# Multiplying each weight slab with both token tiles by turns, with PSUM divided four and four

## The chip, the cores and the metric

The kernel runs on one core of one Trainium2 chip. The metric is the device time of one execution in microseconds (us); less is better.

## The reference

Two transformer blocks over 256 tokens of width 2048, in float32, batch 1. Cut to what matters here:

```
# block 1
h = rms_norm(x);  proj = h @ w_in                       # 7 parts of 1024 columns
o_da = differential_attention(q, k, v)                  # 8 heads, 2 score maps each
o_hg = hgrn2(f, q, i, g)                                # gated linear attention, 8 heads
x = x + rms_norm(concat(o_da, o_hg) @ w_out)
x = x + rms_norm(cross_attention(x, mem) @ w_co)        # 4 heads, 256 memory tokens
x = x + rms_norm((silu(h @ w_gate) * (h @ w_up)) @ w_ffn_out)          # hidden 5632
# block 2
z = rms_norm(x) @ w_in_2                                # pool, q, k, v, gate, r, branch gates
y_a = pool_mixer(p) @ w_branch_a;  y_b = (rms_norm(gla(q, k, v, a)) * silu(r)) @ w_branch_b
x = x + rms_norm((sigmoid(g0) * y_a + sigmoid(g1) * y_b) @ w_out_2)
x = x + rms_norm((silu(h @ w_ffn_gate) * (h @ w_ffn_up)) @ w_ffn_down) # hidden 5632
```

Nearly all work is a product of 256 tokens with a weight matrix that is read once from HBM.

## The kernel before

The 256 tokens are two token tiles of 128, called t = 0 and t = 1 (`NT` is 2). A product is cut into **groups** of 512 weight columns (`group`). A group's weights come in **slabs** of 256 rows by 512 columns (`wsub`): SyncE loads a slab of 512 KB into one of 4 buffers `raw`, ScalarE rounds it to `wh` (line 375), VectorE forms the remainder `wl = raw - wh` (line 376). `wh` and `wl` have 8 buffers each (`SPLIT_BUFS`), so a group over 2048 rows, which is 8 slabs, fills them all. The activations are held transposed and divided in the same way, `hi` and `lo`. TensorE then adds three products for each 128 rows: hi by wh (line 401), hi by wl (402), lo by wh (403); the activation tile is the stationary operand and 512 weight columns stream.

In `mm` one token tile runs over all slabs of the group, then the other: a **pass** for t = 0 and a pass for t = 1, each with a PSUM buffer of its own from the pool `psm` (2 buffers). All other products and transposes take PSUM from the pool `pss` (6 buffers). A slab is free only when the second pass has gone over it.

When a pass is over, a consumer takes the product out of PSUM: `u_in` (line 887, VectorE) multiplies up by silu(gate) into `hh`, `channel` copies to `tok`, `b_in` (lines 1050, 1051) forms the gated branch sum. Most consumers then transpose their tile with 4 products by the identity (line 304, tile `tp`). These steps are generators; `tick`, called after every 6 products of a pass, moves each a step, so that a transpose is written some 6 products behind the pass whose result it takes. The attention parts run in the same way as background jobs between the products.

Engines follow the order in which the tile scheduler places instructions on each; the weights of a group get a priority 50 instructions ahead (`AHEAD`), and none ahead behind a normalisation (`self.bound`, `BOUNDARY_AHEAD`). TensorE, ScalarE and VectorE each take their instructions strictly in that order.

Of the kernel before, what the change touches and what calls it, by code (L numbers as in the profile page):

```python
# [81 lines left out]
class Builder:  # L82
    def __init__(self, ctx, tc, A, out):
        self.tc, self.nc, self.A, self.out = tc, tc.nc, A, out
        e = ctx.enter_context
        self.cp = e(tc.tile_pool(name="const", bufs=1))
        self.ap = e(tc.tile_pool(name="acts", bufs=ACT_UNITS))
        self.rawp = e(tc.tile_pool(name="raw", bufs=RAW_BUFS))
        self.spp = e(tc.tile_pool(name="split", bufs=SPLIT_BUFS))
        self.smp = e(tc.tile_pool(name="small", bufs=16))  # L90
        self.psm = e(tc.tile_pool(name="psm", bufs=2, space=bass.MemoryType.PSUM))
        self.pss = e(tc.tile_pool(name="pss", bufs=6, space=bass.MemoryType.PSUM))
        self.n = 0
        self.junk = self.cp.tile([P, CW], F32, name="junk")
        self.jobs, self.lane, self.bound = [], [], False

# [210 lines left out]
    def split_T(self, ps, gcol=None, same=False):  # L307
        """two float32r parts of ps, each channel times its gain in column gcol (+ i for tile i)."""
        nc = self.nc
        hi, lo = self.uT("hi"), self.uT("lo")  # L310
        if gcol is None:
            nc.scalar.copy(hi, ps)
            nc.vector.tensor_tensor(lo, ps, hi.bitcast(F32), ALU.subtract)
            return hi, lo
        if same:
            g = self.vec[:, gcol:gcol + 1]
            nc.scalar.activation(hi, ps, AF.Copy, scale=g)
            nc.vector.scalar_tensor_tensor(lo, ps, g, hi.bitcast(F32), ALU.mult, ALU.subtract)
            return hi, lo
        for i in range(4):  # L320
            g = self.vec[:, gcol + i:gcol + i + 1]
            nc.scalar.activation(hi[:, i, :], ps[:, i, :], AF.Copy, scale=g)  # L322
            nc.vector.scalar_tensor_tensor(lo[:, i, :], ps[:, i, :], g, hi[:, i, :].bitcast(F32), ALU.mult, ALU.subtract)  # L323
        return hi, lo
# [10 lines left out]
    def token(self, dst, scale):  # L335
        """consumer: token-major, times the token's scale."""
# [6 lines left out]
    def channel(self, dst, scale):  # L343
        """consumer: the same, transposed in float32."""
# [11 lines left out]
    def sigmoid_(self, x):  # L356
        """1/(1+exp(-x)) for an SBUF or PSUM operand, and 1+exp(-x)."""
# [9 lines left out]
    def wsub(self, W, k0, c0, ncol=CW):  # L367
        """256 rows of a weight chunk, split exactly into two float32r parts."""
# [10 lines left out]
    def ahead(self):  # L379
        """weights of a group are prepared before the work emitted just before it; less so behind a boundary."""  # L380
# [4 lines left out]
    def group(self, W, c0, hT, ks, consume, k_off=0, ncol=CW):  # L385
        """out[t] = h[t] @ W[:, c0:c0+ncol] over the k tiles `ks` (even, in pairs)."""
        with self.ahead():
            subs = [(k, self.wsub(W, k + k_off, c0, ncol)) for k in ks[::2]]
        for t in range(NT):
            self.mm(t, subs, hT, consume, ncol)  # L390
# [28 lines left out]
    def normed(self, start, pre):  # L419
        """spawns per token tile: start(t) yields chunks of x; they are transposed, times the gain, and split.  # L420
        Returns rstd and hT, filled as the jobs run."""
# [22 lines left out]
    def residual(self, gain, x, n_chunks=4):  # L444
        """consumers that collect ps*gain and the sum of squares; done(t) yields the chunks of
        x + ps * gain / rms, in the place of ps*gain."""
# [25 lines left out]
    def boundary(self, start, pre):  # L472
        """start(t) -> chunks of the new x, consumed when the last product of tile t is in."""
# [11 lines left out]
    def decay_attn(self, qT, kT, bT, v, esc, cph, dv, store):  # L485
        """qT/kT/bT: per token tile [128 ch, 4, 128]; cph channel tiles per head;
        v(t, head) -> [128 tok, dv]; store(t, h0, ps) takes the outputs."""
# [94 lines left out]
    def head_norm(self, po, nh):  # L582
        """each head of po [128 tok, nh x dv] over its rms; gains are left to the transpose."""
# [15 lines left out]
    def hgrn(self, g, W, hT, rstd, mixT):  # L599
# [42 lines left out]
        self.group(W, 3072 + CW * g, hT, ks, f_in)  # L642
# [80 lines left out]
    def block1(self, x_src):  # L723
# [69 lines left out]
        self.group(A["w_cq"][0], 0, hT, ks, q_in)  # L793
# [60 lines left out]
    def chunks(self, W, hT, ks, cons, job):  # L854
        """all four column chunks of a product with a boundary behind it."""
        for n in range(4):
# [6 lines left out]
            self.group(W, n * CW, hT, ks, g)  # L863

    def ffn(self, x, rstd, hT, Wg, Wu, Wd, post):
        """the feed-forward block; returns done(t), the products of its last consumer, to be given a job."""
# [6 lines left out]
        def run(job):  # L873
            for bi, (b0, nb) in enumerate(blocks):
                hid = [[None] * nb for _ in range(NT)]
                last = bi == len(blocks) - 1
                for c in range(nb):
# [14 lines left out]
                    self.group(Wg, (b0 + c) * CW, hT, ks, g_in)  # L892
# [3 lines left out]
                for n in range(4):  # L896
# [17 lines left out]
                    self.group(Wd, n * CW, hid, list(range(4 * nb)), d_in, k_off=4 * b0)  # L914
        return run, lambda t: self.add_normed(y[t], acc[t], x[t])

# [1 line left out]
    def block2(self, ffn1):  # L918
# [33 lines left out]
        def r_in(a, b, skip):  # L952
            """columns a..b of r, behind `skip` columns of something else."""
# [65 lines left out]
        self.group(W, 5120, hT, ks, gl_in, ncol=416)  # L1019
# [121 lines left out]
```

## Time and profile before

| | |
|---|---|
| time, median of 3 runs | 2907.09 us (2901.22 to 2908.91) |
| span of the profiled execution | 2903.0 us |
| PE (TensorE products) busy | 2844.2 us, 98% |
| PEld (weight loads of TensorE) busy | 2350.3 us, 81% |
| DVE (VectorE) busy | 1616.9 us, 56% |
| ACT (ScalarE) busy | 1412.9 us, 49% |
| moved by DMA | 530.93 MB, mean 183 GB/s |

The profile shows one execution, whose span runs from its first to its last instruction; the time of an execution measured by itself is in the first row, and the span of the profiled one lies within the spread of those. Each engine's row is the time in which it had an instruction in work. A product on PE stands with a modelled end: rows overlap where products are pipelined, so that the pace is read from the starts of rows that follow each other, and an idle time on PE is counted from the modelled end.

### The profile page before, as it was taken

How to read it: one execution, taken by the hardware profiler on the slowest of the kernel's cores; microseconds unless marked ns; L12 is line 12 of the kernel's file. 1: busy time of each engine (PE TensorE's matmuls, PEld its weight loads, DVE VectorE, ACT ScalarE, POOL GpSimd, SP SyncE). 2: the span in 40 equal slices, each digit the busy share in tenths (PEclk: the TensorE clock that was granted, in tenths of full speed). 3: DMA queues.
4: the chain of work that ended last, by engine and by line, in shares of the span. 5: the costliest groups of instructions: out<-in, count | busy, mean ns of one | idle time of the engine just before them, and what ended most of it. 6: DMA issues, size and time to landing. Idle time of an engine off the chain costs nothing.

```text
span 2903.0 us, 35034 instructions
## 1 busy us (share of the span) xinstructions
PE 2844.2 (98%) x13196; PEld 2350.3 (81%) x13196; DVE 1616.9 (56%) x2147; ACT 1412.9 (49%) x2100; POOL 44.8 (2%) x89
## 2 busy tenths in 40 slices
PE   8999999999999999999999999999999999999998
PEld 6788888778888888888888898887887888888887
DVE  6666585664544455447565565555565445444555
ACT  6455584664443443445555475344464344443443
POOL 1000000000000000000000000000000000000000
PEclk9999999999999999999999999999999999999999
DMA  7554456445556556655555446655656556555663
GB/s 227 160 181 159 157 176 206 163 150 182 185 199 196 174 177 204 198 190 192 180 169 165 150 144 212 205 178 178 230 160 214 190 175 191 193 192 177 194 207 136
DMA packets 274921, 530.93 MB, mean 183 GB/s; under 512 B 17513, under 2 KB 29413, under 8 KB 274752
## 3 DMA queue, kind: packets, MB, share of 16 engines
q1 hardware_dynamic: 269040, 512.70, 54.2%
q0 software_dynamic: 5136, 14.95, 1.7%
q8 instruction: 103, 1.69, 0.2%
q10 hardware_dynamic: 576, 1.05, 0.1%
q14 instruction: 66, 0.54, 0.1%
HBM read 522.86 MB, written 5.77 MB: 182 GB/s over the span
## 4 chain that ended last, share of the span: by engine, by line
PE 80%; DMA 7%; DVE 6%; ACT 5%; issue 2%; SPq 0%; ACTq 0%; DVEq 0%
PE mm L401 25%; PE mm L403 25%; PE mm L402 25%; DVE wl L376 3%; ACT wh L375 3%; DMA raw<-w_in 2%; PE tp L304 2%; PE lps L495 1%; DMA raw<-w_ffn_in 1%; DMA raw<-w_ffn_gate 1%; ACT hi L322 1%; ACT junk L299 1%; DVE hh L887 1%; DMA raw<-w_ffn_out 0%; DMA raw<-w_ffn_down 0%
## 5 line engine op out<-in xcount | busy, mean ns | idle before, releaser
L376 DVE TENSOR_TENSOR wl<-raw,wh 128x1024 fp32r<-128x1024 f32 (+1 forms) x968 | 1171.8, 1215 | 728.0 <-ACT wh L375 693.1
L401 PE MATMUL mm<-wh,hi 128*128 128x512 f32 (+2 forms) x3808 | 1497.2, 393 | 6.1 <-ACT hi L322 2.8
L403 PE MATMUL mm<-wh,lo 128*128 128x512 f32 (+2 forms) x3808 | 1482.0, 389 | 0.0
L402 PE MATMUL mm<-wl,hi 128*128 128x512 f32 (+2 forms) x3808 | 1481.6, 389 | 0.0
L375 ACT CAST wh<-raw 128x1024 fp32r<-128x1024 f32 (+1 forms) x968 | 1009.8, 1046 | 793.5 <-PE mm L403 457.7
L401 PEld LDWEIGHTS mm<-wh,hi 128*128 128x128 f32 x3808 | 716.5, 188 | 153.5 <-ACT hi L322 6.7
L403 PEld LDWEIGHTS mm<-wh,lo 128*128 128x128 f32 x3808 | 715.8, 188 | 146.7 <-DVE lo L323 2.1
L402 PEld LDWEIGHTS mm<-wl,hi 128*128 128x128 f32 x3808 | 716.8, 188 | 139.3 <-issue 0.7
L882 ACT ACTIVATE sg<-mm,r 128x512 f32<-128x512 f32 x44 | 30.2, 685 | 168.3 <-PE mm L403 168.3
L887 DVE SCALAR_TENSOR_TENSOR hh<-mm,r,sg 128x512 f32<-128x512 f32 x44 | 32.9, 748 | 131.7 <-PE mm L403 131.7
L333 ACT ACTIVATE tok<-mm,r 128x512 f32<-128x512 f32 x44 | 30.1, 685 | 125.8 <-PE mm L403 125.8
L323 DVE SCALAR_TENSOR_TENSOR lo<-tp,vec,hi 128x128 fp32r<-128x128 f32 x224 | 69.1, 345 | 28.7 <-ACT hi L322 28.1
L322 ACT ACTIVATE hi<-tp,vec 128x128 fp32r<-128x128 f32 x224 | 72.5, 381 | 21.5 <-DVE lo L323 11.5
L906 DVE TENSOR_TENSOR y<-mm,y 128x512 f32<-128x512 f32 x32 | 22.0, 688 | 89.5 <-PE mm L403 89.5
L495 PEld LDWEIGHTS lps<-qd,kd 128*128 128x128 f32 x448 | 58.0, 191 | 4.8 <-DVE qd L522 1.0
L495 PE MATMUL lps<-qd,kd 128*128 128x64 f32 x448 | 56.3, 268 | 0.6 <-DVE qd L522 0.6
L529 DVE COPY_PREDICATED attn<-mask,lps 128x256 f32<-128x256 int32 (+1 forms) x56 | 24.1, 431 | 49.3 <-PE lps L495 49.0
L458 DVE TENSOR_TENSOR mg<-mm,gpost 128x512 f32<-128x512 f32 x24 | 16.5, 686 | 50.2 <-ACT junk L299 50.2
L1042 ACT ACTIVATE gate<-gate 128x512 f32<-128x512 f32 x16 | 10.1, 631 | 68.2 <-DVE gate L1041 68.1
L299 ACT ACTIVATE junk<-mm 128x512 f32<-128x512 f32 x24 | 14.5, 604 | 59.0 <-PE mm L403 59.0
L304 PE MATMUL tp<-ident,hh 128*128 128x128 f32 x176 | 27.6, 279 | 15.2 <-DVE hh L887 15.1
L304 PEld LDWEIGHTS tp<-ident,hh 128*128 128x128 f32 x176 | 20.1, 139 | 27.4 <-DVE hh L887 24.5
(235 smaller groups left out, 1112.8 us busy)
## 6 DMA issues: line engine op xcount, KB each, us to landing
raw<-w_in SPq DMA_DIRECT2D x256, 512.0 KB, 4.6
raw<-w_ffn_in SPq DMA_DIRECT2D x176, 512.0 KB, 4.7
raw<-w_ffn_out SPq DMA_DIRECT2D x88, 512.0 KB, 4.8
raw<-w_ffn_gate SPq DMA_DIRECT2D x88, 512.0 KB, 4.7
raw<-w_ffn_up SPq DMA_DIRECT2D x88, 512.0 KB, 4.7
raw<-w_ffn_down SPq DMA_DIRECT2D x88, 512.0 KB, 4.9
raw<-w_out SPq DMA_DIRECT2D x64, 512.0 KB, 4.9
raw<-w_branch_b SPq DMA_DIRECT2D x32, 512.0 KB, 5.1
```

Source lines behind the costliest of these rows:

```text
L299: self.nc.scalar.activation(self.junk[:, :src.shape[-1]], src, AF.Square, accum_out=acc)
L304: self.nc.tensor.transpose(ps[:, i, :], src[:, i * P:(i + 1) * P], self.ident)
L322: nc.scalar.activation(hi[:, i, :], ps[:, i, :], AF.Copy, scale=g)
L323: nc.vector.scalar_tensor_tensor(lo[:, i, :], ps[:, i, :], g, hi[:, i, :].bitcast(F32), ALU.mult, ALU.subtract)
L375: nc.scalar.copy(hi[:, :, :ncol], raw[:, :, :ncol])
L376: nc.vector.tensor_tensor(lo[:, :, :ncol], raw[:, :, :ncol], hi[:, :, :ncol].bitcast(F32), ALU.subtract)
L401: nc.tensor.matmul(ps[:, :ncol], xh, wh[:, i, :ncol], start=kk == first, stop=False)
L402: nc.tensor.matmul(ps[:, :ncol], xh, wl[:, i, :ncol], start=False, stop=False)
L403: nc.tensor.matmul(ps[:, :ncol], xl, wh[:, i, :ncol], start=False, stop=kk == last)
L495: nc.tensor.matmul(ps[:, h, :], lhs[:, i, :], rhs[:, i, :], start=c == 0, stop=c == cph - 1)
L882: nc.scalar.activation(u, ps, AF.Silu, scale=rstd[t])
L887: nc.vector.scalar_tensor_tensor(u, ps, rstd[t], sg[t], ALU.mult, ALU.mult)
```

## The change

Where `group` ran `mm` twice, it now runs `mm_both`: both token tiles get a PSUM buffer at once, and each slab operand is multiplied with t = 0 and directly after with t = 1. The slab is then done with. Consumers of both tiles are spawned at the end of the group. `tick` still comes after every 6 products. A group keeps the two passes (`apart`) where the second tile's input isn't there yet or a normalisation follows: the first group, the last column group of the products ahead of a normalisation, and the first group behind one. The pool `psm` gets 4 PSUM buffers and `pss` 4. Of 11,616 products with weights, 10,704 are written by `mm_both`.

```
-        self.psm = e(tc.tile_pool(name="psm", bufs=2, space=bass.MemoryType.PSUM))
-        self.pss = e(tc.tile_pool(name="pss", bufs=6, space=bass.MemoryType.PSUM))
+        self.psm = e(tc.tile_pool(name="psm", bufs=4, space=bass.MemoryType.PSUM))
+        self.pss = e(tc.tile_pool(name="pss", bufs=4, space=bass.MemoryType.PSUM))
...
-    def group(self, W, c0, hT, ks, consume, k_off=0, ncol=CW):
+    def group(self, W, c0, hT, ks, consume, k_off=0, ncol=CW, apart=False):
+        apart = apart or self.bound
         with self.ahead():
             subs = [(k, self.wsub(W, k + k_off, c0, ncol)) for k in ks[::2]]
+        if apart:
+            for t in range(NT):
+                self.mm(t, subs, hT, consume, ncol)
+        else:
+            self.mm_both(subs, hT, consume, ncol)
+
+    def mm_both(self, subs, hT, consume, ncol):
+        nc = self.nc
+        ps = [self.psmm() for _ in range(NT)]
+        first, last = subs[0][0], subs[-1][0] + 1
+        for k, (wh, wl) in subs:
+            self.flush(lambda: all(hT[t][k // 4] is not None for t in range(NT)))
+            for i in range(2):
+                kk = k + i
+                for p, w in ((0, wh), (0, wl), (1, wh)):
+                    for t in range(NT):
+                        nc.tensor.matmul(ps[t][:, :ncol], hT[t][kk // 4][p][:, kk % 4, :], w[:, i, :ncol],
+                                         start=kk == first and p == 0 and w is wh, stop=kk == last and p == 1)
+                self.tick()
         for t in range(NT):
-            self.mm(t, subs, hT, consume, ncol)
+            self.spawn(consume(t, ps[t]))
...
-        self.group(W, 3072 + CW * g, hT, ks, f_in)
+        self.group(W, 3072 + CW * g, hT, ks, f_in, apart=g == 0)
...
-            self.group(W, n * CW, hT, ks, g)
+            self.group(W, n * CW, hT, ks, g, apart=n == 3)
```

The same argument is added for the first gate group of a feed-forward block, the last column group of its output product, the query product of the cross attention and the first group of block 2.

On TensorE, where one group ends and the next begins, in the feed-forward block of block 1. Before, this is the end of an up group's second pass (product `mm_1348`), then the first pass of the next gate group (`mm_1377`), and in it the transposes of the tile `hh_1352` that the second pass gave:

```order
L402 MATMUL mm_1348_6228<-wl_1345_6174,hi_1249_5718 128x512
L403 MATMUL mm_1348_6228<-wh_1344_6173,lo_1250_5719 128x512
L401 MATMUL mm_1377_6336<-wh_1354_6290,hi_1184_5450 128x512
L402 MATMUL mm_1377_6336<-wl_1355_6291,hi_1184_5450 128x512
L403 MATMUL mm_1377_6336<-wh_1354_6290,lo_1185_5451 128x512
L401 MATMUL mm_1377_6336<-wh_1354_6290,hi_1184_5450 128x512
L402 MATMUL mm_1377_6336<-wl_1355_6291,hi_1184_5450 128x512
L403 MATMUL mm_1377_6336<-wh_1354_6290,lo_1185_5451 128x512
L304 MATMUL tp_1378_6343<-ident_81,hh_1352_6286 128x128 x4
```

The same place in the changed kernel (`mm_1346` and `mm_1347` are the two tiles of the up group, `mm_1374` and `mm_1375` of the next, `hh_1348` and `hh_1349` what the consumer makes of the first two):

```order
L407 MATMUL mm_1346_6177<-wh_1344_6173,lo_1195_5513 128x512
L407 MATMUL mm_1347_6178<-wh_1344_6173,lo_1250_5719 128x512
L407 MATMUL mm_1374_6327<-wh_1351_6281,hi_1184_5450 128x512
L407 MATMUL mm_1375_6328<-wh_1351_6281,hi_1241_5660 128x512
L407 MATMUL mm_1374_6327<-wl_1352_6282,hi_1184_5450 128x512
L407 MATMUL mm_1375_6328<-wl_1352_6282,hi_1241_5660 128x512
L407 MATMUL mm_1374_6327<-wh_1351_6281,lo_1185_5451 128x512
L407 MATMUL mm_1375_6328<-wh_1351_6281,lo_1242_5661 128x512
L304 MATMUL tp_1376_6335<-ident_81,hh_1348_6275 128x128 x4
L304 MATMUL tp_1377_6340<-ident_81,hh_1349_6277 128x128 x4
```

The transposes still stand 6 products into the next group, but now those of both token tiles, and the products between take each slab operand twice in a row.

On VectorE, around the consumers of the same up group. Before, between the first tile's `hh_1347` and the second's `hh_1352`, with `wl_1355` to `wl_1376` the eight slabs of the next group and `lo` the remainder of a transposed tile:

```order
L887 SCALAR_TENSOR_TENSOR hh_1347_6226<-mm_1346_6177,r_1203_5548,sg_1319_6076 128x512
L376 TENSOR_TENSOR wl_1355_6291<-raw_1353_6288,wh_1354_6290 128x1024
L313 TENSOR_TENSOR lo_1351_6247<-tp_1349_6235,hi_1350_6246 128x512
L376 TENSOR_TENSOR wl_1358_6297<-raw_1356_6294,wh_1357_6296 128x1024
L376 TENSOR_TENSOR wl_1361_6303<-raw_1359_6300,wh_1360_6302 128x1024
L376 TENSOR_TENSOR wl_1364_6309<-raw_1362_6306,wh_1363_6308 128x1024
L376 TENSOR_TENSOR wl_1367_6315<-raw_1365_6312,wh_1366_6314 128x1024
L376 TENSOR_TENSOR wl_1370_6321<-raw_1368_6318,wh_1369_6320 128x1024
L887 SCALAR_TENSOR_TENSOR hh_1352_6286<-mm_1348_6228,r_1256_5750,sg_1321_6127 128x512
L376 TENSOR_TENSOR wl_1373_6327<-raw_1371_6324,wh_1372_6326 128x1024
```

In the changed kernel (`wl_1352` to `wl_1373` are the eight slabs of the next group):

```order
L376 TENSOR_TENSOR wl_1364_6306<-raw_1362_6303,wh_1363_6305 128x1024
L376 TENSOR_TENSOR wl_1367_6312<-raw_1365_6309,wh_1366_6311 128x1024
L376 TENSOR_TENSOR wl_1370_6318<-raw_1368_6315,wh_1369_6317 128x1024
L908 SCALAR_TENSOR_TENSOR hh_1348_6275<-mm_1346_6177,r_1203_5548,sg_1320_6125 128x512
L908 SCALAR_TENSOR_TENSOR hh_1349_6277<-mm_1347_6178,r_1256_5750,sg_1321_6127 128x512
L376 TENSOR_TENSOR wl_1373_6324<-raw_1371_6321,wh_1372_6323 128x1024
L313 TENSOR_TENSOR lo_1379_6352<-tp_1376_6335,hi_1378_6351 128x512
L313 TENSOR_TENSOR lo_1381_6356<-tp_1377_6340,hi_1380_6355 128x512
```

The two consumers now stand side by side, behind seven of the next group's eight slabs; before, six slabs stood between them.

On TensorE in the differential attention of the changed kernel: `atp_715` is a transposed score tile, `aT_716` what ScalarE copies from it, `tp_723` a transposed memory tile; with four buffers in `pss`, `tp_723` takes the PSUM buffer that `atp_715` had.

```order
L714 MATMUL atp_715_3347<-ident_81,sce_661_3171 128x128 x2
L407 MATMUL mm_703_3297<-wh_701_3293,hi_17_148 128x512
L407 MATMUL mm_704_3298<-wh_701_3293,hi_70_357 128x512
L407 MATMUL mm_703_3297<-wl_702_3294,hi_17_148 128x512
L407 MATMUL mm_704_3298<-wl_702_3294,hi_70_357 128x512
L407 MATMUL mm_703_3297<-wh_701_3293,lo_18_149 128x512
L407 MATMUL mm_704_3298<-wh_701_3293,lo_71_358 128x512
L304 MATMUL tp_723_3379<-ident_81,mem_710_3337 128x128 x4
L723 MATMUL dapo_670_3209<-tok_454_2226,aT_716_3350 128x128 x2
```

Six products lie between the last write of the old tile and the first write of the new one. In the program before there are 3 places in `pss` with room for at most 12 products between (other work of TensorE counted by its columns); in the changed one 12.

## Rows read from the trace of the kernel before

**Rows 1.** The page: span, and its first part (busy, share, instructions).
```profile
span 2903.0 us, 35034 instructions
PE 2844.2 (98%) x13196; PEld 2350.3 (81%) x13196; DVE 1616.9 (56%) x2147; ACT 1412.9 (49%) x2100; POOL 44.8 (2%) x89
```
**Rows 2.** Groups of PE by form: count, busy us, mean ns, idle before, releasers.
```profile
L401 PE MATMUL mm<-wh,hi 128*128 128x512 f32 x3648 | 1440.0, 395 | 5.7 <-ACT hi L322 2.4 <-DVE mg L458 1.8 <-ACT wh L375 1.0
```
**Rows 3.** Timeline of PE around a change of pass: start, duration, instruction.
```profile
1012.88 0.39 PE L402 MATMUL mm<-wl,hi 128*128 128x512 f32 x1
1013.10 0.39 PE L403 MATMUL mm<-wh,lo 128*128 128x512 f32 x1
1013.33 0.39 PE L401 MATMUL mm<-wh,hi 128*128 128x512 f32 x1
...
1014.46 0.39 PE L403 MATMUL mm<-wh,lo 128*128 128x512 f32 x1
1014.70 0.60 PE L304 MATMUL tp<-ident,hh 128*128 128x128 f32 x4
```
**Rows 4.** Windows: a first pass and a second pass; busy us of each engine.
```profile
1002.50:1013.50 11.00, 11.00 (x50) 9.13 (x49) 3.67 (x3) 2.83 (x4) 0.00 (x0) 1.00 0.66 222
1013.50:1024.50 11.00, 11.00 (x52) 9.06 (x52) 7.48 (x7) 6.52 (x7) 0.00 (x0) 1.00 0.50 163
```
**Rows 5.** Timeline of ACT in the next second pass; in brackets idle before and releaser.
```profile
1041.10 1.06 ACT L375 CAST wh<-raw 128x1024 fp32r<-128x1024 f32 x1 [0.30 <-PE mm L403]
1042.46 1.06 ACT L375 CAST wh<-raw 128x1024 fp32r<-128x1024 f32 x1 [0.30 <-PE mm L403]
1044.46 1.05 ACT L375 CAST wh<-raw 128x1024 fp32r<-128x1024 f32 x1 [0.95 <-DMA raw<-w_ffn_in]
```
**Rows 6.** Waits of PE, whole span: total us, times, longest.
```profile
PE tp L304 <- DVE hh L887: 15.1, 20, 1.5
...
PE tp L304 <- DVE gate L1051: 4.6, 4, 1.7
PE tp L304 <- DVE sg L946: 3.0, 2, 2.1
...
PE tp L304 <- ACT tok L333: 2.6, 4, 1.1
PE cpo L821 <- ACT tok L333: 2.2, 1, 2.2
...
PE tp L304 <- DVE hn L594: 1.3, 2, 1.1
PE mm L401 <- ACT wh L375: 1.0, 1, 1.0
```
**Rows 7.** Timeline of all engines at the end of an up group's second pass.
```profile
1069.69 1.05 ACT L375 CAST wh<-raw 128x1024 fp32r<-128x1024 f32 x1 [2.39 <-DMA raw<-w_ffn_out]
...
1070.77 1.23 DVE L376 TENSOR_TENSOR wl<-raw,wh 128x1024 fp32r<-128x1024 f32 x1 [2.22 <-ACT wh L375]
...
1071.08 0.39 PE L403 MATMUL mm<-wh,lo 128*128 128x512 f32 x1
...
1071.91 0.74 DVE L887 SCALAR_TENSOR_TENSOR hh<-mm,r,sg 128x512 f32<-128x512 f32 x1
...
1072.71 0.66 PE L304 MATMUL tp<-ident,hh 128*128 128x128 f32 x4 [1.24 <-DVE hh L887]
```
**Rows 8.** DVE timeline, the consumer of a first pass.
```profile
1013.53 0.75 DVE L887 SCALAR_TENSOR_TENSOR hh<-mm,r,sg 128x512 f32<-128x512 f32 x1 [6.70 <-PE mm L403]
```
**Rows 9.** Tile gate: the two steps of the branch sum, ns min/median/max.
```profile
L1050 DVE TENSOR_TENSOR gate<-mm,gate x8: 682/688/691, 1911.4 to 2062.4; 128x512 f32<-128x512 f32 x8
L1051 DVE TENSOR_TENSOR gate<-gate,gate x8: 681/689/693, 1912.1 to 2064.7; 128x512 f32<-128x512 f32 x8
```
**Rows 10.** Waits of TensorE's weight loads: for a copied score tile.
```profile
PEld dapo L702 <- ACT aT L695: 0.9, 3, 0.5
```
**Rows 11.** A window near the start (before the last two columns: granted clock), and PE in it.
```profile
25.00:30.00 5.00, 4.94 (x23) 4.20 (x24) 3.95 (x11) 4.62 (x14) 3.94 (x8) 0.66 0.97 346
...
26.18 0.57 PE L402 MATMUL mm<-wl,hi 128*128 128x512 f32 x1
26.55 0.63 PE L403 MATMUL mm<-wh,lo 128*128 128x512 f32 x1
```

More of the change, by code (lines that the diff above doesn't have):

```diff
@@ L792, in q_in @@
             yield from self.channel(cqT, rq)(t, ps)
-        self.group(A["w_cq"][0], 0, hT, ks, q_in)
+        self.group(A["w_cq"][0], 0, hT, ks, q_in, apart=True)
         oT = [[None] for _ in range(NT)]
@@ L891, in u_in @@
                         yield from self.to_T(u, put)
-                    self.group(Wg, (b0 + c) * CW, hT, ks, g_in)
+                    self.group(Wg, (b0 + c) * CW, hT, ks, g_in, apart=bi == 0 and c == 0)
                     self.group(Wu, (b0 + c) * CW, hT, ks, u_in)
@@ L913, in d_in @@
                                 self.spawn(job(t))
-                    self.group(Wd, n * CW, hid, list(range(4 * nb)), d_in, k_off=4 * b0)
+                    self.group(Wd, n * CW, hid, list(range(4 * nb)), d_in, k_off=4 * b0, apart=last and n == 3)
         return run, lambda t: self.add_normed(y[t], acc[t], x[t])
@@ L1017, in unit @@
                 self.group(W, 3072 + n * CW, hT, ks, self.token(vs[n], rstd))
-        self.group(W, 5120, hT, ks, gl_in, ncol=416)
+        self.group(W, 5120, hT, ks, gl_in, ncol=416, apart=True)
         unit(0)
```

## Prediction

> **What bounds the kernel now.** I read the first part of the page first: PE is busy for 98% of the span, VectorE and ScalarE for about half of it [rows 1]. A product's row lasts 0.39 us while the next one starts 0.23 us later [rows 3], so that busy share counts overlap. The starts tell the pace: from 1012.88 to 1014.46 lie 7 steps, 1.58 us, or 0.226 to 0.227 us for each product of 512 columns. 10,944 of them (3 lines of 3648 [rows 2]) make 0.227 x 10,944 = 2,484 us of a span of 2,903; the rest of the 11,616 are like them, and transposes and attention products come on top. TensorE's own work is therefore the bound, and this change removes none of it. What can be gained is the time in which PE waits, what can be lost are new waits or a slower pace.
>
> So I read the waits of PE next. The largest is that of transposes for `hh`, what VectorE makes of an up product: 15.1 us in 20 places; then `gate` 4.6, `sg` 3.0, `tok` 2.6, one wait of the cross attention 2.2, and for slabs themselves 1.0 [rows 6]. A feed-forward block has 11 up groups, two blocks 22, two passes each: 20 waits in 44 transposed tiles means that about one tile of each group waits.
>
> The windows and timelines say which and why. In a first pass VectorE works 3.7 of 11 us and ScalarE 2.8; in the second pass after it 7.5 and 6.5 [rows 4]. All eight slab buffers are held until the second pass goes over them, so that the next group's slabs are made in a burst: ScalarE waits for a release by TensorE every 1.36 us, and when the loaded buffers are used up, for the next load [rows 5]. The end of such a pass shows the price: at 1069.69 ScalarE gets a late slab, its remainder holds VectorE from 1070.77 to about 1071.9, only then comes `hh`, 0.8 us behind the pass's last product at 1071.08, and the transposes start at 1072.71 after 1.24 us of idle PE [rows 7]. The waiting tile is that of the second pass. The first pass's `hh` starts at 1013.53, 0.20 us after the next pass began, takes 0.75 and is ready 0.4 us ahead of its transposes at 1014.70 [rows 3, 8].
>
> **The change part by part.**
>
> *Products.* Their number, operands and columns stay. Two things alternate now: the PSUM bank, and the stationary tile. The trace has the bank switch: 1013.10 is the last product of one bank and 1013.33 the first of another, 0.23 us like its neighbours [rows 3]. It has the stationary switch too: hi by wh and hi by wl share the stationary tile, lo by wh does not, and the steps are alike [rows 3]. Cost 0. Unknown is only whether many switches in a row act as one does: a rival below.
>
> *Slabs.* A slab is used 12 times in a row and then free, one each 12 x 0.227 = 2.7 us instead of eight in a burst of 1.36 us each. ScalarE needs 1.05 us for one and VectorE 1.23 [rows 5, 7], and no load has to land faster than every 2.7 us. The wait for slabs, 1.0 [rows 6], goes: -1 us.
>
> *Transposes of `hh`.* Each idle in the list is counted from a modelled end. Where nothing waits, transposes start 0.24 us after the last product's start [rows 3]; at 1071.08 they start 1.63 us after, so 1.39 are lost where the list counts 1.24 [rows 7]: 0.15 more for each. 15.1 + 20 x 0.15 = 18.1 us are there to be gained. What replaces it, with 0 the start of the next group's first product: the first tile's last product is now one earlier, so its `hh` can start at 0.20 - 0.23 = -0.03. Ahead of it on VectorE stands the remainder of the seventh slab (the order shows it): its buffer comes free one slab early, at -2.7; with 0.3 for the release [rows 5], 1.05 and 1.23 it ends at about -0.1. So the first `hh` lies at 0 to 0.75, the second to 1.5, and the transposes are due at 6 x 0.227 = 1.36 and 0.35 later, 1.7. Both are in time by 0.2 to 0.6. I leave 1 us of 18 for places where a load is late: -17 us. Bounds: 0 if VectorE is late as now, -18.
>
> *Transposes of `gate`.* 4.6 + 4 x 0.15 = 5.2 us of waits [rows 6]. Two tiles take 2 x (0.69 + 0.69) = 2.8 us on VectorE [rows 9]; the order now writes these transposes 14 products behind the group's end, 14 x 0.227 = 3.2 us, where it had 7. -5 us; bounds 0 and -5.2.
>
> *Transposes of `sg`, `tok` and `hn`.* 6.9 us in 8 places [rows 6]. They wait for chains of ScalarE and VectorE which the end of the bursts helps, and which now hold both tiles at once. I take -2; bounds +7 and -8.
>
> *Cross attention.* Its values are needed from both tiles; both copies now come after the group's last product, so that the wait of 2.2 [rows 6] grows by one more tile's share of ScalarE, not above its 0.7 us: +1 us.
>
> *Four PSUM buffers instead of six for the rest.* Twelve places have at most 12 products of room between the old tile's last write and the new one's first, where three had. The nearest wait in the trace is that for a copied score tile, 0.9 us in 3 [rows 10]: 12 x 0.3 = +4 us. Lower bound 0; upper, if at each a slab's rounding of 1.05 us [rows 5] stands ahead of the copy, 12 x 1.35 = +16.
>
> *Groups kept apart, start and end.* Their order is as before; 0.
>
> Sum: -1 - 17 - 5 - 2 + 1 + 4 = -20 us. The span of the profiled run, 2903.0, lies 4 us under the median of the timed runs; I take the difference from the median: 2907 - 20 = **2887 us**.
>
> **The rivals.**
>
> *The waits stay (no change).* VectorE could be late at a group's end as it is now, then the second `hh` would come 0.75 us behind the first and wait in turn. For it: VectorE's order still has slabs ahead of the pair. Against it: a slab is due only every 2.7 us, and VectorE is busy 56% [rows 1]. Without the 17 us of `hh`, and the 2 of `sg`, the sum is -1: 2906 us.
>
> *The alternation costs pace (slower).* Place: each of the 10,704 products written by turns. 3 ns more on each is 32 us, and 2907 - 20 + 32 = 2919; it decides from 2 to 3 ns on. Against it stand the single switch at 0.23 and the stationary switch in every third product [rows 3]. The worse form is a falling clock: between 25 and 30 us, where the granted clock averages 0.66, products start 0.37 us apart [rows 11], 0.14 over the pace; one product in twenty like that is 535 x 0.14 = +75 us, 2962. [...]
>
> *The alternation gains pace (much faster).* If a part of the 0.227 were the wait of one accumulation for the one before in the same bank, taking turns would remove it. With 10 ns on each of 10,704 that is 107 us: 2780. Against it: the first product into a new bank at 1013.33 starts no sooner than others [rows 3]. [...]
>
> *Four buffers starve the attention (slower).* With waits not at 12 places but at 36, at 1.35 us each, +49 instead of +4: 2932 us. It decides from 24 us on, 18 such waits. For it: the attention's stages hold two score tiles, a transposed one and two outputs at once, more than four. Against it: ScalarE and VectorE are half idle.
>
> **How the numbers follow.** Chances: the forecast 0.69, waits stay 0.16, alternation costs pace 0.05, gains pace 0.03, attention starved 0.07. The forecast's own range is from -36 (all bounds at their low end) to -9: 2871 to 2898. A measurement of this kernel tells about 0.3% (9 us) from no change. Faster takes the forecast and the gained pace, with 0.01 from the others: 0.73; same 0.16; slower 0.11. The range leaves out the far rivals on both sides, 0.03 and about 0.10, and reaches over the case that waits stay: 2866 to 2908.
>
> **What would show it.** Right: PE's waits for `hh` and `gate` nearly gone from the list; ScalarE's slab castings 2.7 us apart over the whole group, VectorE and ScalarE equally busy in its halves; steps of 0.227 between products; no new wait in the attention stages above some us. Wrong: steps of 0.23 or more between products that take turns; a row of waits of transposes or score products for tiles of `pss`; `hh` still behind a late slab.

## The result, and the profile after

| | before | changed |
|---|---|---|
| time, median (lowest to highest) | 2906.07 us (2901.22 to 2908.91), 4 runs | 2867.47 us (2866.83 to 2868.51), 4 runs |
| span of the profiled execution | 2903.0 us | 2866.7 us |

The ratio is 0.9871 (95%: 0.9857 to 0.9885). The change takes 38.6 us off: faster, as forecast, by about twice the 20 us of the sum and at the lower edge of the range (2866 to 2908).

The page of the changed kernel, its span and first part, answers to [rows 1]:

```profile
span 2866.7 us, 35013 instructions
PE 2836.1 (99%) x13196; PEld 2351.4 (82%) x13196; DVE 1619.9 (57%) x2147; ACT 1412.8 (49%) x2100; POOL 44.7 (2%) x89
```

Every engine does the work that it did: the counts are the same. Of the 36.3 us by which the span is shorter, 28.2 are idle time of PE and 8.1 busy time; around a wait products also overlap less, which the modelled ends count as busy (the 0.15 us of the prediction at each place, read at 1072.71 [rows 7] and an estimate for the others). PE's waits over the whole span (in total, times, longest) are the answer to [rows 6]:

```profile
PE tp L304 <- DMA x<-x: 5.3, 4, 3.1
PE tp L304 <- DVE vec L181: 3.6, 1, 3.6
...
PE tp L304 <- DVE hh L908: 1.8, 1, 1.8
PE cpo L842 <- ACT tok L333: 1.4, 2, 0.8
...
PE mm L422 <- ACT hi L322: 0.9, 4, 0.4
PE tp L304 <- DVE hn L615: 0.5, 2, 0.3
...
PE mm L423 <- DVE wl L376: 0.2, 1, 0.2
```

`hh` is left at one place of twenty. `gate`, `sg` and `tok` (as a wait of transposes) are gone from the list. One wait is new: near the start, a transpose stands 3.6 us for `vec`, the copy that frees a PSUM buffer of `pss`; what it costs is taken up in the part on the prediction. All rows of the list sum to 47.8 us in 52 places before and 19.1 in 19 after: 28.7 less. With the 0.15 us that the list misses at each place (the same estimate), 33 places fewer are 5.0 more, together 33.7 of the 36.3 us between the two spans. The other 2.6 stay unassigned.

The three timelines and the windows that follow show why. First ScalarE's of the changed kernel, around the end of a group (start, duration, instruction; in brackets idle before and releaser), beside [rows 5]:

```profile
1007.41 1.05 ACT L375 CAST wh<-raw 128x1024 fp32r<-128x1024 f32 x1 [1.67 <-PE mm L407]
...
1012.85 1.05 ACT L375 CAST wh<-raw 128x1024 fp32r<-128x1024 f32 x1 [1.67 <-PE mm L407]
1015.57 1.06 ACT L375 CAST wh<-raw 128x1024 fp32r<-128x1024 f32 x1 [1.67 <-PE mm L407]
```

The row left out, at 1010.13, is like the others. A slab every 2.72 us (12 products of 0.227), each released by TensorE and none by a load; before they came 1.36 us apart, until the loaded buffers were used up. Over the whole span ScalarE's castings of slabs stand 37 times for a load, 25.6 us in all; in the kernel before it was 324 times and 299 us. Windows of a group's two halves (busy us of PE, PEld, DVE, ACT, POOL) beside [rows 4]:

```profile
993.00:1004.00 11.00, 11.00 (x50) 9.13 (x49) 5.02 (x5) 5.38 (x6) 0.00 (x0) 1.00 0.66 195
1004.00:1015.00 11.00, 11.00 (x50) 9.09 (x50) 5.02 (x5) 4.22 (x4) 0.00 (x0) 1.00 0.66 196
```

VectorE's 5.02 and 5.02 stand where 3.67 and 7.48 stood. VectorE's timeline at the end of that group, then PE's at the same place, beside [rows 3, 7, 8]:

```profile
1013.94 1.22 DVE L376 TENSOR_TENSOR wl<-raw,wh 128x1024 fp32r<-128x1024 f32 x1 [1.49 <-ACT wh L375]
1015.35 1.41 DVE L908 SCALAR_TENSOR_TENSOR hh<-mm,r,sg 128x512 f32<-128x512 f32 x2 [0.18 <-PE mm L407]
1016.67 1.22 DVE L376 TENSOR_TENSOR wl<-raw,wh 128x1024 fp32r<-128x1024 f32 x1
```

```profile
1014.92 0.61 PE L407 MATMUL mm<-wh,lo 128*128 128x512 f32 x2
1015.37 0.62 PE L407 MATMUL mm<-wh,hi 128*128 128x512 f32 x2
1015.83 0.62 PE L407 MATMUL mm<-wl,hi 128*128 128x512 f32 x2
1016.28 0.62 PE L407 MATMUL mm<-wh,lo 128*128 128x512 f32 x2
1016.74 1.03 PE L304 MATMUL tp<-ident,hh 128*128 128x128 f32 x8
```

The next group starts at 1015.37. The remainder ahead of the consumers is done at 1015.16, 0.2 us before that; both `hh` run from 1015.35 to 1016.76; the eight transposes go without a wait from 1016.74. The six products from 1015.37 to 1016.74 take 0.228 us each, the pace of before.

### The profile page after: what moved, and what is told of

It is laid out like the page before. It is cut to its first block, busy times and chain, and to the rows that moved or that the text cites. A ratio compares the mean times of both kernels' runs of the same rounds, so it can differ in the third digit from the quotient of the medians.

```text
span 2866.7 us, 35013 instructions
## 1 busy us (share of the span) xinstructions
PE 2836.1 (99%) x13196; PEld 2351.4 (82%) x13196; DVE 1619.9 (57%) x2147; ACT 1412.8 (49%) x2100; POOL 44.7 (2%) x89
## 4 chain that ended last, share of the span: by engine, by line
PE 94%; ACT 2%; DMA 1%; DVE 1%; issue 1%; SPq 0%; DVEq 0%; ACTq 0%
PE mm L407 83%; PE tp L304 2%; PE lps L516 2%; PE mm L422 2%; PE mm L423 2%; PE mm L424 2%; ACT junk L299 1%; ACT hi L322 1%; DVE wl L376 1%; DMA raw<-w_ffn_in 1%; ACT wh L375 0%; PE po L581 0%; PE sc L686 0%; DMA raw<-w_in 0%; DMA x<-x 0%
## 5 line engine op out<-in xcount | busy, mean ns | idle before, releaser
L407 PE MATMUL mm<-wh,hi 128*128 128x512 f32 (+1 forms) x3504 | 1091.5, 392 | 0.0
L407 PE MATMUL mm<-wl,hi 128*128 128x512 f32 (+1 forms) x3504 | 1080.0, 389 | 0.0
L407 PE MATMUL mm<-wh,lo 128*128 128x512 f32 (+1 forms) x3504 | 1077.6, 388 | 0.0
L407 PEld LDWEIGHTS mm<-wh,hi 128*128 128x128 f32 x3504 | 648.6, 188 | 129.9 <-issue 5.8
L422 PE MATMUL mm<-wh,hi 128*128 128x512 f32 (+1 forms) x304 | 121.6, 400 | 1.4 <-ACT hi L322 0.9
L423 PE MATMUL mm<-wl,hi 128*128 128x512 f32 (+1 forms) x304 | 120.1, 395 | 0.3 <-DVE wl L376 0.2
L424 PE MATMUL mm<-wh,lo 128*128 128x512 f32 (+1 forms) x304 | 119.8, 394 | 0.0
L323 DVE SCALAR_TENSOR_TENSOR lo<-tp,vec,hi 128x128 fp32r<-128x128 f32 x224 | 68.3, 345 | 15.9 <-ACT hi L322 15.1
L422 PEld LDWEIGHTS mm<-wh,hi 128*128 128x128 f32 x304 | 57.8, 190 | 16.5 <-ACT hi L322 6.5
L333 ACT ACTIVATE tok<-mm,r 128x512 f32<-128x512 f32 x44 | 30.1, 690 | 33.6 <-PE mm L407 33.6
L312 ACT CAST hi<-tp 128x512 fp32r<-128x512 f32 x54 | 29.6, 589 | 21.5 <-PE tp L304 21.4
L535 DVE TENSOR_TENSOR e<-b 128x512 f32<-128x512 f32 x56 | 38.3, 683 | 0.0
```

The costliest lines, as they stand in the source:

```text
L407: nc.tensor.matmul(ps[t][:, :ncol], hT[t][kk // 4][p][:, kk % 4, :], w[:, i, :ncol], start=kk == first and p == 0 and w is wh, stop=kk == ...
L422: nc.tensor.matmul(ps[:, :ncol], xh, wh[:, i, :ncol], start=kk == first, stop=False)
L423: nc.tensor.matmul(ps[:, :ncol], xh, wl[:, i, :ncol], start=False, stop=False)
L424: nc.tensor.matmul(ps[:, :ncol], xl, wh[:, i, :ncol], start=False, stop=kk == last)
L535: nc.vector.tensor_tensor(ev, bv, bv[:, :, hh - 1:hh].to_broadcast([P, 4 * nb, 2 * hh]), ALU.subtract)
```

## The experiments

The theory to test: the gain comes from the order in which slabs come free. Released one by one, every 2.72 us, they ask for loads, roundings and remainders at that rate. Released in a second pass, eight at 1.36 us, they outrun the loads; a late load then holds ScalarE and VectorE, and the pass's consumer stands behind the held slab in VectorE's order, as in [rows 7], where `hh` starts 0.83 us after the pass's last product. The rivals: the other parts of the change (both consumers at the group's end with more products ahead of their transposes; the PSUM division; the bank that alternates) bring or cost the time. Each time is a median, with the median of the kernel before from the same series in parentheses; that one lay between 2898 and 2907 us in the series, so that the ratio is what counts.

**Only the PSUM pools** (the kernel before).

```diff
-        self.psm = ... name="psm", bufs=2
-        self.pss = ... name="pss", bufs=6
+        self.psm = ... name="psm", bufs=4
+        self.pss = ... name="pss", bufs=4
```

> The kernel before (one token tile over the whole group, then the other), with PSUM divided four and four as in the changed kernel. Theory A (the gain comes from slabs that come free one by one, so that VectorE and ScalarE no longer make eight in a burst just when a pass's result is due): no gain, 2900 to 2912 us, the waits of transposes for hh still 15 to 18 us on PE; if four buffers starve the attention, up to 15 us slower than before. Rival B (two more PSUM buffers for products are what helps): near the changed kernel, 2870 us.

Measured: 2898.9 us (2899.52), 1.0001 (0.9992 to 1.0009). PE's waits, this kernel:

```profile
PE tp L304 <- DVE hh L887: 7.8, 14, 1.2
...
PE tp L304 <- DVE gate L1051: 5.6, 4, 2.0
```

The division of PSUM alone neither gains nor costs anything that can be measured. One part of the expectation failed: `hh` waits 7.8 us in this execution, not the 15 to 18 expected. The rows of the list sum to 42.0 us, against 47.8 in the execution of [rows 6], which is of another series, with a median 6.6 us longer. Whether the kernel before waits as little for `hh` in a series like this one isn't known: only one execution of it was profiled.

**Both banks, but one token tile over all slabs, then the other** (the changed kernel; consumers of both tiles at the group's end as in the change).

```diff
-        for k, (wh, wl) in subs:
-            self.flush(lambda: all(hT[t][k // 4] is not None for t in range(NT)))
-            for i in range(2):
-                kk = k + i
-                for p, w in ((0, wh), (0, wl), (1, wh)):
-                    for t in range(NT):
+        for t in range(NT):
+            for k, (wh, wl) in subs:
+                self.flush(lambda: hT[t][k // 4] is not None)
+                for i in range(2):
+                    kk = k + i
+                    for p, w in ((0, wh), (0, wl), (1, wh)):
```

> The changed kernel with its two PSUM buffers per group and both consumers at the group's end, but one token tile runs over all slabs and then the other, so that slabs come free in a burst as before. Theory A: the second tile's hh still stands in the burst; since the first tile's transposes now come just ahead of its own, it has 0.35 us more room in each of 22 groups, 8 us: 2890 to 2902 us. Rival D (what helps is that both consumers and both transposes come together at the end of a group): 2867 to 2872 us.

Measured: 2897.65 us (2899.52), 0.9993 (0.9984 to 1.0001). PE's waits, this kernel:

```profile
PE tp L304 <- DVE gate L1072: 6.5, 4, 2.4
...
PE tp L304 <- DVE hh L908: 4.8, 13, 0.9
PE tp L304 <- DVE sg L967: 4.5, 3, 2.4
PE tp L304 <- ACT tok L333: 3.9, 6, 1.2
```

With everything of the change but the order of the products, the whole gain is gone and the waits are back, `gate`, `sg` and `tok` in full and `hh` in part. This one edit is worth 1.2%, about 31 to 35 us. It isn't quite only the release of slabs: the scheduler also places the transposes of `gate` nearer to the group's end here, 6 and 10 products behind it instead of 14 as in the change. Those of `hh` stand 6 behind in both.

**Turns of three products instead of one** (the changed kernel): all three products of 128 rows for one tile, then for the other.

```diff
-                for p, w in ((0, wh), (0, wl), (1, wh)):
-                    for t in range(NT):
+                for t in range(NT):
+                    for p, w in ((0, wh), (0, wl), (1, wh)):
```

> The changed kernel with turns of three products instead of one: for each 128 rows the three products of t = 0, then the three of t = 1. The slab is done with at the same time as in the changed kernel. Theory A: 2864 to 2872 us, as the changed kernel, steps between products 0.227. Rival C (taking turns product by product changes TensorE's pace, through the PSUM bank, the stationary tile or the slab that streams twice in a row): turns a third as often would move the time by more than 5 us.

Measured: 2865.63 us (2899.52), 0.9879 (0.9866 to 0.9892), as the changed kernel. PE's timeline in it:

```profile
1000.03 0.39 PE L407 MATMUL mm<-wh,lo 128*128 128x512 f32 x1
1000.26 0.39 PE L407 MATMUL mm<-wh,hi 128*128 128x512 f32 x1
1000.48 0.39 PE L407 MATMUL mm<-wl,hi 128*128 128x512 f32 x1
```

Steps of 0.22 to 0.23 us here too. Whether bank and stationary tile alternate with every product or with every third makes no difference here (0.9871 and 0.9879 of the kernel before); what both kernels share is that a slab is done with before the next one.

**Transposes written 12 products behind instead of 6** (the kernel before), in `to_T`: room for a late consumer without touching the slabs.

```diff
-        yield 1
+        yield 2
```

> The kernel before, with every consumer's transposes written six products (1.36 us) later, and nothing else. Theory A in its narrow form (what is lost is only that results are late for transposes, by at most the 1.5 us of the longest wait for hh): waits for hh, gate and tok go, 2875 to 2885 us, with slabs still in bursts. Rival (the bursts cost TensorE more than that, in the pace of products or in waits for slabs): 2895 us or more.

Measured: 2913.87 us (2899.52), 1.0051 (1.0039 to 1.0063): slower, and the wait for `hh` is longer than ever, 19.4 us. ScalarE's, VectorE's and PE's timeline at one place:

```profile
760.20 1.05 ACT L375 CAST wh<-raw 128x1024 fp32r<-128x1024 f32 x1 [1.60 <-DMA raw<-w_ffn_in]
...
761.29 1.23 DVE L376 TENSOR_TENSOR wl<-raw,wh 128x1024 fp32r<-128x1024 f32 x1 [1.43 <-ACT wh L375]
...
762.43 0.74 DVE L887 SCALAR_TENSOR_TENSOR hh<-mm,r,sg 128x512 f32<-128x512 f32 x1
...
763.23 0.66 PE L304 MATMUL tp<-ident,hh 128*128 128x128 f32 x4 [1.34 <-DVE hh L887]
```

The expectation of 2875 to 2885 us failed. That more room is what helps is refuted in this form: the consumer's place on VectorE moved back with its transposes. Between the two `hh` of the group quoted in the part on the change VectorE now has seven slabs where it had six, and the row at 760.20 shows the last slab ahead of `hh` held by a load for 1.60 us. Room in the code of TensorE was no room here, where the order of VectorE is made from it. But the place alone isn't what costs: in the next experiment seven slabs stand there too, loads are late less often, and `hh` waits 1.2 us.

**Five buffers for loads instead of four** (the kernel before; `ACT_UNITS` gives up two units of memory for it).

```diff
-RAW_BUFS = 4
-ACT_UNITS = 54
+RAW_BUFS = 5
+ACT_UNITS = 52
```

> The kernel before with five buffers for loaded slabs instead of four (and 52 buffers for activations instead of 54, to make the room). Theory A': in a burst, late loads hold ScalarE and VectorE, and the second tile's hh stands behind the held slab; with one more slab loaded ahead the burst ends earlier and hh is in time: 8 to 18 us faster than before, waits for hh under 8 us. Rival (VectorE's and ScalarE's own work in the burst is too much, loads or not): within 5 us of before.

Measured: 2879.74 us (2898.18), 0.9936 (0.9923 to 0.9948): 18.4 us less, about half of the change's gain, without any change of the products' order. ScalarE's timeline in a second pass, then PE's waits:

```profile
1038.96 1.06 ACT L375 CAST wh<-raw 128x1024 fp32r<-128x1024 f32 x1 [0.30 <-PE mm L403]
1041.39 1.05 ACT L375 CAST wh<-raw 128x1024 fp32r<-128x1024 f32 x1 [1.37 <-DMA raw<-w_ffn_in]
```

```profile
PE tp L304 <- ACT tok L333: 3.7, 3, 3.0
...
PE tp L304 <- DVE sg L946: 3.0, 2, 2.3
...
PE tp L304 <- DVE gate L1051: 1.8, 2, 1.4
```

The burst still runs, but only its last slab waits for a load (over the whole span 131 slabs and 107 us, against 324 and 299). `hh` is no longer among the long waits (1.2 us in 4 places); `sg` and part of `gate` are, as chains on engines that work through a burst.

**Three buffers for loads**, in the kernel before and in the changed one.

```diff
-RAW_BUFS = 4
+RAW_BUFS = 3
```

> The kernel before with three buffers for loaded slabs instead of four. A buffer's round (load 4.7, rounding 1.05, remainder 1.23, 7 us) over three buffers is 2.3 us a slab, where the burst asks for one in 1.36. Theory A': the burst gets longer by 8 x 0.5 us and every group's second-pass results and the next group's slabs come late: 30 us slower than before or more. Rival (loads are not what holds the burst): within 10 us of before.

> The changed kernel with three buffers for loaded slabs instead of four. Theory A': 2.3 us a slab is still under the 2.7 us at which slabs come free, so that the time stays within 8 us of the changed kernel, except at the groups kept apart. Rival (the changed kernel too lives on loads ahead): 20 us or more over the changed kernel.

Measured: before 2922.74 us, changed 2886.28 us (both beside 2898.18): 1.0079 (1.0061 to 1.0097) and 0.9956 (0.9942 to 0.997). The kernel before loses 24.6 us, less than the 30 expected, and the changed one about 20 (its own median lies near 2866), which is the figure of the rival. The expectation that the changed kernel would hardly mind outside the groups kept apart gave no size for those; about half of the loss arises behind two of them. Two rows of PE's waits, the first of the kernel before and the second of the changed one with three buffers:

```profile
PE mm L402 <- DVE wl L376: 2.8, 5, 0.8
```

```profile
PE tp L304 <- DVE hh L908: 6.9, 2, 3.7
```

The two waits of the changed kernel end at 668.25 and 2188.51 us, in the first up group of each feed-forward block, behind a gate group kept apart: there eight slabs still come free in a burst. Of the 18.0 us by which its last product with weights lies behind that of the changed kernel, 9.5 arise around these two places. In the groups by turns of these blocks nothing is lost: the distance stays at 6.3 us from 691 to 1342 us and at 18.0 from 2204 us to the end. So with late loads the changed kernel pays in these blocks where the burst is left, and not elsewhere. The kernel before doesn't follow its expectation so well. Not every group loses: against its profile with four buffers, 17 us are lost by 669 us, about where the first feed-forward block begins, and 4 in all the rest, and `hh` waits 10.9 us in total, less than in [rows 6]. Why is open.

**Two and three PSUM buffers for products** (the changed kernel).

```diff
-... name="psm", bufs=4      ... name="pss", bufs=4
+... name="psm", bufs=2      ... name="pss", bufs=6     # then 3 and 5
```

> The changed kernel with PSUM divided two and six, as before. The next group's first products then wait for the consumer of the same bank: 0.2 us to its start and 0.7 us of work for the first tile, up to 0.7 more for the second, in about 110 groups written by turns. Theory A (the even release is the gain, and four buffers for products are what it takes not to lose it again): 100 to 180 us over the changed kernel, 2965 to 3045 us. Rival (two buffers do, the consumers being quick): within 20 us of the changed kernel.

> The changed kernel with three PSUM buffers for products and five for the rest. The next group's first tile has a free bank, its second must wait for the consumer of the group before: the first tile's bank comes free about 0.75 us after the group's end, and the second tile's first product is due 0.23 after it. Some 0.5 to 0.7 us in each of 110 groups: 50 to 80 us over the changed kernel. Rival (the waits cost nothing, since VectorE and ScalarE take the first bank at once): within 15 us.

Measured: with two 2986.17 us (2898.18), 1.03 (1.0284 to 1.0317); with three 2875.68 us (2907.15), 0.9894 (0.9879 to 0.991). PE's waits with two, then with three:

```profile
PE mm L407 <- DVE hh L908: 14.9, 21, 0.7
...
PE mm L407 <- ACT sg L903: 11.0, 20, 0.6
```

```profile
PE mm L407 <- DVE hh L908: 2.5, 2, 1.5
```

With two, the next group's products wait for a consumer to empty their bank, 21 times for `hh` and 20 times for `sg` in 22 up and 22 gate groups, up to 0.7 us each, and TensorE stands: without the PSUM division the change loses 3%. With three, 50 to 80 us were expected to be lost, and it is only 9. So the division is needed for the change, though alone it gives nothing, and three of the four buffers carry nearly all of it.

**All groups by turns, none kept apart** (the changed kernel).

```diff
-        apart = apart or self.bound
+        apart = False
```

> The changed kernel with every group by turns, those at a normalisation too. The first token tile's sum of squares, normalisation and transposes then start at the end of the group and not half a group (11 us) before it, and the next group's first products need both tiles' new input. At six places some 5 to 11 us of that work are no longer covered: 25 to 65 us over the changed kernel. Rival (the scheduler finds other work for TensorE there): within 10 us.

Measured: 2891.31 us (2907.15), 0.9949 (0.9935 to 0.9963): 25 us more than the change, at the low end of what was expected. PE's waits:

```profile
PE tp L304 <- DVE mg L490: 10.6, 3, 4.8
PE tp L304 <- DVE yg L490: 4.9, 1, 4.9
```

Ahead of a normalisation the first tile's chain of ScalarE and VectorE has no second pass to hide under. That the groups at these places stay apart is part of the gain.

**The changed kernel again, and with five buffers for loads** and the first vectors' product moved from `pss` to `psm`.

```diff
-RAW_BUFS = 4
-ACT_UNITS = 54
+RAW_BUFS = 5
+ACT_UNITS = 52
...
-        ps = self.ps("vecps")
+        ps = self.psmm("vecps")
```

> The changed kernel once more, beside the runs of before on this chip, as the measure for the others of this call: 0.986 to 0.989 of before.

> The changed kernel with five buffers for loaded slabs (52 for activations) and the start's transposed gain vector in a PSUM buffer of the products, so that the fifth of the first transposes need not wait for it. Theory A': the loads hold the changed kernel only behind groups kept apart (one wait for hh of 1.8 us, boundary waits of some 0.3 us), and the start wait for the vector of 3.6 us partly stands in place of one for loads: 2 to 7 us under the changed kernel. Rival (the even release and the fifth buffer gain separately, as the fifth buffer alone gained 18 us): 12 us or more under it.

Measured: 2866.26 us, 0.9861 (0.9843 to 0.9879), and 2861.8 us, 0.9847 (0.9831 to 0.9863), both beside 2907.15. The second is the fastest of all, 4.5 us below the change; its longest execution, 2864.03 us, lies below the shortest of the change, 2865.76. PE's waits in it:

```profile
PE tp L304 <- DMA x<-x: 4.6, 4, 2.4
PE tp L304 <- ACT tok L333: 3.5, 1, 3.5
```

The wait for `vec` is gone from the list, and so is that for `hh`; a wait of 3.5 us for `tok` at one place is new. The two edits weren't run apart. Of the 4.3 us between the two profiled spans, 3.0 are there by 145 us, and the next part shows that the moved product gains nothing at the start, so that the fifth buffer is the likelier cause; that isn't shown.

## Why the prediction was right, and where it was too small

**The bound and the pace**: right. Products start 0.226 to 0.227 us apart before [rows 3] and 0.227 after (12 of them to a slab, a slab every 2.72 us); the rivals on the pace, whose prices were 32, 75 and 107 us, don't occur, neither with one product to a turn nor with three (0.22 to 0.23 us). The 3 and the 10 ns on each product that two of these prices stand for show in no run. The third was a falling clock: the granted clock is 1.00 in both windows of the group shown above and 0.998 in the mean of the whole run, against 0.997 before, so that the 10,704 products written by turns, whose banks alternate, show no loss of clock.

**`hh`, -17**: the mechanism and the size are right. 15.1 us in 20 places are 1.8 in one, 16.1 less with 0.15 for each place. The working held to a tenth of a microsecond: the consumers begin 0.02 us ahead of the next group (forecast 0.03), the slab ahead of them ends 0.21 ahead (forecast 0.1), the transposes come 1.37 behind (forecast 1.36). The remaining wait, at 662.85 us, is in the first up group, behind a group kept apart.

**Slabs, -1**: right, 0.8.

**`gate`, -5**: the number is right, 5.2, the reason isn't. The prediction has the transposes 14 products behind the group's end "where it had 7". Seven is the distance of the first tile's, which didn't wait. Those that waited are the second tile's, and they stood 16 or 17 products behind their pass, further than now. In the kernel before, with the pass's last product at 1922.43:

```profile
1923.20 0.68 DVE L1050 TENSOR_TENSOR gate<-mm,gate 128x512 f32<-128x512 f32 x1
...
1924.97 1.05 ACT L375 CAST wh<-raw 128x1024 fp32r<-128x1024 f32 x1 [0.84 <-DMA raw<-w_in]
...
1926.05 1.23 DVE L376 TENSOR_TENSOR wl<-raw,wh 128x1024 fp32r<-128x1024 f32 x1 [0.66 <-ACT wh L375]
...
1927.19 0.68 DVE L1051 TENSOR_TENSOR gate<-gate,gate 128x512 f32<-128x512 f32 x1
...
1927.93 0.66 PE L304 MATMUL tp<-ident,gate 128*128 128x128 f32 x4 [1.26 <-DVE gate L1051]
```

In the changed kernel, 14 products behind the group's end:

```profile
1903.62 1.26 PE L304 MATMUL tp<-ident,gate 128*128 128x128 f32 x8
```

The second step of the branch sum stood behind slabs whose loads were late, as `hh` did. That the term came out is luck: it is the same cause as for `hh`, and the room counted for it was there before.

**`sg`, `tok` and `hn`, -2**: this term failed in size. The three lost 3.3, 3.2 and 0.8 us, 7.3 together, close to the lower bound of -8. The prediction granted the end of the bursts a part of these waits. For `sg` and `tok` it took them whole: in the run with one tile after the other they stand at 4.5 and 3.9 us again. `hn` waits 0.5 us in that run too, as in the changed kernel, so its 0.8 belong to another part of the change.

**The small waits, 0 in the sum**: the second failure in size. Rows of 0.2 to 7 us which the sum left out (loads of `x`, `hi`, `mg`, `lps`, `f` and others) lost 7.3 us by the two lists, with 0.15 for each place that is gone. The prediction counted the rows that it named and took the rest as fixed. One of them, 1.8 us of products for `mg`, is gone in both kernels that have four buffers for products and the old release order as well (that with only the pools changed, and that with one tile after the other): that is the PSUM division. Another, 2.1 us of products for `hi` at the start, comes up again below. For the others no run separates what the release order moved from what differs between any two executions.

**Cross attention, +1**: wrong in sign. The wait of 2.2 became two of 1.4 together; less waiting ahead of the group may outweigh the second copy behind it, but no run shows that.

**Four buffers for the rest, +4**: no price shows. At the twelve places of the attention nothing of it stands in PE's list. The one new wait, 3.6 us for `vec`, is at the start, where the sum had put 0, and it stands in place of another. The first product with weights of the changed kernel, then of the kernel before, then of the kernel with five load buffers where `vec` comes from `psm`:

```profile
13.15 0.80 PE L422 MATMUL mm<-wh,hi 128*128 128x512 f32 x1
```

```profile
13.63 0.79 PE L401 MATMUL mm<-wh,hi 128*128 128x512 f32 x1 [2.11 <-ACT hi L322]
```

```profile
13.93 0.79 PE L422 MATMUL mm<-wh,hi 128*128 128x512 f32 x1 [2.46 <-ACT hi L322]
```

Where TensorE doesn't wait for `vec`, it waits for the first `hi`, and starts no earlier. In the kernel with only the pools changed the wait for `vec` is 2.2 us, that product starts at 13.33, and no time is lost in all.

By terms, then: -0.8 for slabs, -16.1, -5.2, -7.3 and -0.7 make -30.1, the small waits with the new one -3.6, and 2.6 are unassigned: 36.3 us between the spans. The remaining 2.3 to the 38.6 of the medians is where the two profiled executions lie in their series. The gain is larger than the sum by the terms at -2, +1 and +4 and by the small waits.

**The range**: its lower end is partly luck. The bounds of the terms add up to about -31, not to the -36 that the prediction gives for them; by them the lowest time is 2876 us, and the measured 2867.5 lies some 8 below. It is inside because the stated range goes down to 2866, and no term stands for that last part.

**The rivals**: "the waits stay" failed for the changed kernel, but it is what happens when the same consumers follow two whole passes (2897.65 us). "Four buffers starve the attention" didn't occur; it is buffers for products, not for the rest, that can starve (2986 us with two).

What stays open: how much of the gain is the late load itself and how much the burst on ScalarE and VectorE, and how much of it comes by way of the scheduler, which moves some transposes with the release order. A fifth load buffer in the kernel before removes 18.4 us, which is the part of loads as far as one more buffer reaches; in the burst that is left `tok`, `sg` and `gate` go on waiting. A kernel in which loads are never late but slabs still come in a burst wasn't run, nor one with a ninth slab buffer.

## What to carry to other kernels

Where several consumers share a buffer, run the loop so that one buffer's last use comes before the next buffer's first use: the same work per buffer then asks its producers for an even rate, here a slab every 2.72 us instead of eight 1.36 us apart. That beat one more load buffer with the old order (2866 us against 2880). It cost a result buffer more for each consumer in flight: with two PSUM buffers instead of four the change lost (2986 us). A wait of the bound engine for one engine's tile can be caused two steps up, by a load that holds the instruction ahead of it in that engine's order (with the transposes 12 products behind, a load held ScalarE for 1.60 us and TensorE then waited 1.34 for `hh`), so read what that engine did just before. When summing what a release order gives, count all waits downstream of the producers that it unburdens, not the largest row alone. And before a new wait gets a price, look when the work behind it starts: one wait can take the place of another, as the 3.6 us for `vec` took that of the 2.1 for `hi`.

## What the runs showed of the hardware that was not expected

The same bytes landed sooner where they were asked for evenly. DMA issues on the changed kernel's page (count, size, median us from issue to landing):

```profile
raw<-w_ffn_in SPq DMA_DIRECT2D x176, 512.0 KB, 3.8
```

The kernel before has 4.7 us for the same 176 loads, with 183 GB/s on average in place of 185; the run with one tile after the other, which differs in the order of products alone, has 4.7 too, and the kernel before with five buffers 5.2. And the changed kernel's time was steadier: the kernel before had medians from 2898.18 to 2907.15 us in different series, the changed one 2867.47 and 2866.26; in the last of these series nine executions of before lie 11.9 us apart and four of the changed kernel 1.4.
